# Taking the last 32 of 256 tokens out of the dense expert products of a PEER layer, and turning the output product

## The chip, the cores and the metric

The kernel runs on one core of one Trainium2 chip. The metric is the device time of one launch in microseconds (us), the median of several runs. The engines are TensorE (PE; PEld is its weight load), VectorE (DVE), ScalarE (ACT), GpSimd (POOL), and SyncE (SP), whose queue issues most DMAs.

## The reference

Two layers, each a trunk (attention, convolution and recurrence heads over 256 tokens of 1024 columns) and then a PEER mixer over 16384 experts of one neuron each. Only the mixer is touched by the change:

```python
def peer(xn, wq, k1, k2, u_tab, v_tab):
    q = (xt @ wq).reshape(t, PEER_HEADS, D_KEY)          # 8 heads
    ...
    v1, i1 = lax.top_k(s1, TOPK)                         # 16 of 128 keys, twice
    v2, i2 = lax.top_k(s2, TOPK)
    ...
    sv, ci = lax.top_k(cand, TOPK)                       # 16 of the 256 pairs
    experts = (e1 * N_KEYS + e2)                         # 128 experts a token
    gates = jax.nn.softmax(sv, axis=-1)
    ...
    hid = jax.nn.gelu(jnp.einsum("td,tkd->tk", xi, u_tab[ei]))
    return jnp.einsum("tk,tkd->td", gi * hid, v_tab[ei])
```

So each token needs the rows of 128 experts out of `u_tab` and out of `v_tab`. All is float32.

## The kernel before

**Dense instead of gathered.** The kernel multiplies all 256 tokens with all 16384 rows of `u` and of `v`, and a matrix of gates, zero where an expert was not chosen, stands between the two. A weight block is 128x1024 float32 (512 KB). `load` (L151, on SP's queue) brings it into one of three `raw` buffers; `split` makes of it two parts that TensorE takes at full rate, `hi` on ScalarE (L163) and `lo` on VectorE (L164), in three buffers each. `fixed_weight` (L168 to L174) multiplies the block with the 256 tokens: for each of eight 128x128 pieces hi by XH, hi by XL, and lo by XH, 24 matmuls of 256 columns.

**Stages of one layer's mixer.** Sixteen such blocks make the queries (`wq`), and scores with the keys come out of them. A list of tasks then finds the experts: `first_level` (L629, top 16 of 128, with `top16` L623 to L627), `second_prep` (L670), `second_level`, `decode_ranks` (L686 to L702), `decode_index`, `decode_sum` (L710, L717 to L721), `gates` and `turn` (L740 to L752, the transposed expert numbers `eH`, `eT` and gates `gT`), each for two halves `tt` of 128 tokens. Nearly all of it is VectorE's. The tasks are dealt out over the first J1 = 36 blocks of `u` (`hpair`, two blocks each). The other 92 blocks run beside 64 `quad`s: one quad builds, by comparisons on VectorE (L776, L782) and scaled copies on ScalarE and VectorE (L789, L792), one-hot matrices for four tokens and multiplies them in eight float16 matmuls (L798) into these tokens' columns of the gate matrix in `ab`. `hpair` also takes the gelu and the product with the gates.

Then comes the V stage: 128 `out_step`s, one for each block of `v`. ScalarE (L846) and VectorE (L847) split the coefficients of the block into two parts `chl`, which are the stationary operand here; `accumulate` (L250 to L252) runs 12 matmuls of 512 columns of `v` with them into four PSUM banks, which hold the output with tokens on partitions. `add_rows` adds the residual and takes the norm's sums.

**What sets the order.** The source is written in the order of these loops, but the instructions of each engine are ordered when the kernel is built, by a scheduler that may take an instruction earlier than it stands in the source when its inputs are there; `split` has a raised priority. Each engine then runs its own list in that order.

In the names below, `lo`, `hi`, `raw` are the block's parts, `ab` is the large buffer with the gates, the coefficients and the tasks' scratch, `cst` are constants.

Of the kernel before, what the change touches and what calls it, by code (L numbers as in the profile page):

```python
# [7 lines left out]
F32 = mybir.dt.float32  # L8
# [9 lines left out]
P = 128  # L18
# [17 lines left out]
CW = 661  # L36
# [9 lines left out]
def hymba_peer_kernel(  # L46
# [11 lines left out]
    v_in: bass.AP,  # L58
    g1_in: bass.AP,
# [15 lines left out]
    WARM=12,  # L75
):
# [25 lines left out]
    ab = one.tile([P, P * T], F32, name="ab")  # L102
    ab3 = ab.rearrange("p (n t) -> p n t", t=T)
# [37 lines left out]
    # products of zeros: the tensor engine's clock is up when the first rows arrive  # L141
# [44 lines left out]
    def add_rows(tt, ps, gb):  # L186
        # the residual, its rows' scales, and its product with the gains
# [76 lines left out]

    def log1p_exp_neg_abs(dst, z, n, tag):
# [3 lines left out]
        # exp(-|z|) = ((1 - t) / (1 + t)) ** 4 with t = tanh(|z| / 8)  # L269
# [8 lines left out]
        # log1p(e) = 2 atanh(e / (2 + e))  # L278
# [10 lines left out]
    def trunk(l, mx_p, prev, gb):  # L289
# [44 lines left out]
        # values and forget gates, in the layout [token, column]  # L334
# [41 lines left out]
        # log(1 + exp(-|z|)) of the forget gates and of the recurrence's lambda  # L376
# [9 lines left out]
        # cumulative log forget gates as rank-two terms of the logits  # L386
# [29 lines left out]
        # conformer convolution  # L416
# [19 lines left out]
        def layer_norm():  # L436
# [16 lines left out]
            # a Newton step: y (1.5 - 0.5 v y^2)  # L453
# [10 lines left out]
        # gated linear recurrence  # L464
# [30 lines left out]
        def rnn_scan():  # L495
            # -expm1(2 log_a) = tanh(-log_a) (1 + a^2)
# [10 lines left out]
            # sqrt(v) = v y (1.5 - 0.5 v y^2)  # L507
# [11 lines left out]
        # attention  # L519
# [61 lines left out]
        # output projection and residual  # L581
# [11 lines left out]
        return wq  # L593

    def peer(l, oh_p, wq, next_gain):
        o = 16384
# [22 lines left out]
        gT = oh_p.tile([P, 2, T], F32, name="gT", bufs=1)  # L619

# [83 lines left out]
        def decode_index(tt, s):  # L704
            # sum over ranks a of (a == chosen rank) * index[a]
# [31 lines left out]
        def turn(tt):  # L737
# [7 lines left out]
            # the scaled gate as two float16 parts, each kept as float32  # L745
# [8 lines left out]
        for tt in range(2):  # L754
# [11 lines left out]
            tasks.append((1.0, lambda tt=tt: turn(tt)))  # L766

# [41 lines left out]
        def hpair():  # L809
            j = jc[0]  # L810
            b = bank()
            fixed_weight(u_in[l, j], b[:, 0:T])
            fixed_weight(u_in[l, j + 1], b[:, T:2 * T])
            bv = b.rearrange("p (n t) -> p n t", t=T)
# [3 lines left out]
            else:  # L818
                hg = oh_p.tile([P, 2, T], F32, tag="hg", name="hg")
# [21 lines left out]
        def out_step(j):  # L841
            def f():
                chl = oh_p.tile([P, 2, T], F32R, tag="hg", name="chl")
# [6 lines left out]
                return (chl[:, 0, :], chl[:, 1, :]), w  # L850
# [11 lines left out]
        pr = [bankb() for _ in range(4)]  # L862
# [128 lines left out]
```

## Time and profile before

| | us |
|---|---|
| median of 3 runs | 1882.45 (1881.66 to 1882.49) |
| span of the profiled execution | 1879.8 |
| TensorE busy | 1850.7 (98%) |
| VectorE busy | 1358.5 (72%) |
| ScalarE busy | 1196.0 (64%) |
| POOL busy | 28.1 (1%) |
| mean DMA rate | 175 GB/s |

The profile comes from one execution. Its page gives busy time by engine, the chain of work that ended last, groups of instructions by line, and the DMA issues; the trace behind it can be asked for windows, single instructions and the chain in a stretch. A matmul's shown duration contains its way through the array, so the time from one start to the next, not the duration, tells how fast matmuls follow each other.

### The profile page before, as it was taken

The page shows a single profiled execution, that of the slowest core. Times are in us where ns is not written, and L with a number is a line of the kernel's source. Part 1 is how long each engine was busy: PE and PEld are TensorE (multiplying, and loading weights), DVE is VectorE, ACT ScalarE, POOL GpSimd, SP SyncE. Part 2 cuts the span into 40 slices and gives each one's busy share as a digit, 9 for nine tenths or more (in the row PEclk, how much of TensorE's full clock was granted, in tenths as well). Part 3 has the DMA queues.
Part 4 walks back from the last instruction along what each step waited for, and adds up shares of the span by engine and source line. Part 5 has one row for each costly group of instructions (what it writes and reads, how often), then busy time and mean ns, then how long its engine had stood idle before and what let it go on. Part 6 is the DMA issues. An engine that isn't in the chain of part 4 may idle for free.

```text
span 1879.8 us, 33413 instructions
## 1 busy us (share of the span) xinstructions
PE 1850.7 (98%) x12688; PEld 1672.3 (89%) x12688; DVE 1358.5 (72%) x2902; ACT 1196.0 (64%) x2345; POOL 28.1 (1%) x34
## 2 busy tenths in 40 slices
PE   9999999999999999999999999999999999999998
PEld 8889999999998888888897899999999988888886
DVE  6969987778885555555688699777788755555555
ACT  5954668888874444444469455598888744444444
POOL 0100000000000000000010000000000000000000
PEclk9999999999999999999999999999999999999999
DMA  6264555555555655555543545655555565555554
GB/s 228 91 210 154 168 184 168 160 167 166 163 166 202 211 188 186 188 190 188 184 156 118 174 152 172 193 160 166 168 159 169 167 213 191 186 187 189 190 190 136
DMA packets 90016, 328.86 MB, mean 175 GB/s; under 512 B 9984, under 2 KB 9984, under 8 KB 89600
## 3 DMA queue, kind: packets, MB, share of 16 engines
q1 hardware_dynamic: 88704, 322.54, 52.8%
q10 hardware_dynamic: 1152, 4.19, 0.6%
q8 instruction: 99, 1.62, 0.3%
q14 instruction: 61, 0.50, 0.1%
HBM read 323.55 MB, written 3.15 MB: 174 GB/s over the span
## 4 chain that ended last, share of the span: by engine, by line
PE 89%; DVE 8%; ACT 2%; issue 1%; POOL 0%; DMA 0%; POOLq 0%; SPq 0%; ACTq 0%
PE bank L172 14%; PE bank L174 14%; PE bank L173 14%; PE bankb L251 13%; PE bankb L250 13%; PE bankb L252 13%; PE bankb L798 3%; DVE lo L164 3%; PE bank L651 1%; DVE ab L627 1%; DVE ab L625 1%; DVE ab L626 1%; DVE ab L624 1%; PE bank L231 0%; DVE ab L623 0%
## 5 line engine op out<-in xcount | busy, mean ns | idle before, releaser
L164 DVE TENSOR_TENSOR lo<-raw,hi 128x1024 fp32r<-128x1024 f32 (+1 forms) x600 | 734.1, 1225 | 255.6 <-ACT hi L163 252.1
L163 ACT ACTIVATE hi<-raw 128x1024 fp32r<-128x1024 f32 (+1 forms) x600 | 630.5, 1053 | 262.8 <-PE bank L173 126.3
L172 PE MATMUL bank<-XH,hi 128*128 128x256 f32 x2560 | 732.0, 286 | 0.0
L174 PE MATMUL bank<-XH,lo 128*128 128x256 f32 x2560 | 723.0, 282 | 6.2 <-DVE lo L164 6.2
L173 PE MATMUL bank<-XL,hi 128*128 128x256 f32 x2560 | 719.5, 281 | 0.7 <-DVE XL L236 0.7
L174 PEld LDWEIGHTS bank<-XH,lo 128*128 128x128 f32 x2560 | 483.0, 189 | 8.4 <-DVE lo L164 8.2
L172 PEld LDWEIGHTS bank<-XH,hi 128*128 128x128 f32 x2560 | 484.4, 189 | 1.4 <-issue 0.4
L173 PEld LDWEIGHTS bank<-XL,hi 128*128 128x128 f32 x2560 | 483.5, 189 | 1.1 <-DVE XL L236 1.1
L250 PE MATMUL bankb<-hi,chl 128*128 128x512 f32 x1024 | 406.1, 397 | 1.0 <-ACT chl L846 1.0
L251 PE MATMUL bankb<-lo,chl 128*128 128x512 f32 x1024 | 405.5, 396 | 0.0
L252 PE MATMUL bankb<-hi,chl 128*128 128x512 f32 x1024 | 405.3, 396 | 0.0
L846 ACT ACTIVATE chl<-ab 128x256 fp32r<-128x256 f32 x256 | 106.7, 418 | 361.7 <-PE bankb L252 361.7
L789 ACT ACTIVATE ob<-oe,gT 128x128 f16<-128x128 f16 x768 | 251.9, 407 | 0.9 <-DVE oe L782 0.9
L250 PEld LDWEIGHTS bankb<-hi,chl 128*128 128x128 f32 x1024 | 192.7, 188 | 48.7 <-ACT chl L846 2.4
L252 PEld LDWEIGHTS bankb<-hi,chl 128*128 128x128 f32 x1024 | 192.1, 188 | 47.3 <-DVE chl L847 0.7
L251 PEld LDWEIGHTS bankb<-lo,chl 128*128 128x128 f32 x1024 | 192.6, 188 | 45.4
L847 DVE SCALAR_TENSOR_TENSOR chl<-ab,chl 128x256 fp32r<-128x256 f32 x256 | 108.9, 426 | 157.9 <-ACT chl L846 157.9
L776 DVE TENSOR_TENSOR oa<-iota,eH 128x512 f16<-128x512 f16 x128 | 54.2, 424 | 50.1 <-PE bankb L798 49.3
L798 PE MATMUL bankb<-ob,oa 128*128 128x128 f16 x1024 | 74.0, 222 | 0.0
L792 DVE TENSOR_SCALAR ob<-iota_h,eT,gT 128x128 f16<-128x128 f16 x256 | 70.6, 310 | 0.0
L782 DVE TENSOR_TENSOR oe<-iota,eH 128x512 f16<-128x512 f16 x128 | 53.9, 424 | 20.6 <-ACT ob L789 19.7
L798 PEld LDWEIGHTS <-oa 128*128 128x128 f16 x1024 | 60.2, 115 | 4.0
(198 smaller groups left out, 1171.4 us busy)
## 6 DMA issues: line engine op xcount, KB each, us to landing
raw<-in_u_dram SPq DMA_DIRECT2D x256, 512.0 KB, 3.5
raw<-in_v_dram SPq DMA_DIRECT2D x256, 512.0 KB, 4.2
raw<-in_ws_dram SPq DMA_DIRECT2D x32, 512.0 KB, 3.6
raw<-in_wq_dram SPq DMA_DIRECT2D x32, 512.0 KB, 4.0
raw<-in_wo_dram SPq DMA_DIRECT2D x16, 512.0 KB, 3.8
raw<-in_wv_dram SPq DMA_DIRECT2D x8, 528.0 KB, 3.7
ab<-in_g_dram SPq DMA_DIRECT2D x4, 512.0 KB, 5.8
ab<-in_kt_dram SPq DMA_DIRECT2D x2, 1024.0 KB, 6.7
```

The costliest lines, as they stand in the source:

```text
L163: S.activation(out=hi, in_=r, func=AF.Copy)
L164: V.tensor_tensor(out=lo, in0=r, in1=hi.bitcast(F32), op=ALU.subtract)
L172: TE.matmul(out=ps, lhsT=hi[:, k, :], rhs=XH[:, k, :], start=(k == 0), stop=False)
L173: TE.matmul(out=ps, lhsT=hi[:, k, :], rhs=XL[:, k, :], start=False, stop=False)
L174: TE.matmul(out=ps, lhsT=lo[:, k, :], rhs=XH[:, k, :], start=False, stop=(k == KT - 1))
L250: TE.matmul(out=po, lhsT=mh, rhs=hi[:, d0:d0 + 512], start=(m == 0), stop=False)
L251: TE.matmul(out=po, lhsT=mh, rhs=lo[:, d0:d0 + 512], start=False, stop=False)
L252: TE.matmul(out=po, lhsT=ml, rhs=hi[:, d0:d0 + 512], start=False, stop=(m == n - 1))
L789: S.activation(out=ob[:, s, i, :], in_=oe[:, :, i], func=AF.Copy, scale=gT[:, s, t:t + 1])
L798: TE.matmul(out=b[:, i * P:(i + 1) * P], lhsT=oa[:, :, i], rhs=ob[:, s, i, :], start=(s == 0), stop=(s == 1))
L846: S.activation(out=chl[:, 0, :], in_=c, func=AF.Copy, scale=1.0 / GS)
L847: V.scalar_tensor_tensor(out=chl[:, 1, :], in0=c, scalar=1.0 / GS, in1=chl[:, 0, :].bitcast(F32), op0=ALU.mult, op1=ALU.subtract)
```

## The change

For the last TG = 32 tokens the dense products are left out; TD = 224 tokens stay dense.

- `fixed_weight` on `u` blocks takes 224 columns of XH and XL; there are 56 quads instead of 64; `ab` holds 128 x 224 columns.
- `gathered_rows` lays the 32 tokens' normed rows out so that partition 32 g + t holds token t (`hG`, four copies). `gathered_index` makes expert numbers `idx` and gates `gG` in the same layout: on partition 32 g + t, column i, is expert 32 g + i of token t.
- `gathered_dot(i)`: an indirect DMA on POOL (L689) fetches, for each of the 128 partitions, the row of `u` of its expert in column i (4 KB a row, 512 KB in all) into one of NROW = 3 buffers; VectorE multiplies with `hG` and sums along the row into `cG` (L695). `gathered_gelu` applies gelu and gates. `gathered_sum(i)` fetches rows of `v` in the same way and adds them, scaled by `cG`, to `aG` (L707, L709). There are 32 dots and 32 sums a layer; the source places the dots among the 92 blocks of `u` and the sums among the steps of V.
- V is transposed: `accumulate_turned` has the pieces of `v` as the stationary operand, and for each of eight of them one matmul of 448 columns (hi with both parts of the coefficients) and one of 224 (lo). They fill all eight PSUM banks. At the end `finish` adds the two parts, transposes back, and adds `aG` by a matmul that sums the four groups.
- The tasks run for `tt` = 1 first, since the 32 tokens are in that half.

```diff
+    def accumulate_turned(ot, steps, tail, finish):
...
+            TE.matmul(out=ot[d][:, 0:2 * TD], lhsT=hi[:, w],
+                      rhs=chl.rearrange("p s t -> p (s t)"), start=(m == 0), stop=False)
+            TE.matmul(out=ot[d][:, 0:TD], lhsT=lo[:, w], rhs=chl[:, 0, :], start=False,
+                      stop=(m == n - 1))
...
+        def gathered_rows():
...
+            for dh in range(2):
+                b = bank()
+                TE.matmul(out=b, lhsT=dr, rhs=xg[:, dh * 512:(dh + 1) * 512],
+                          start=True, stop=True)
+                S.activation(out=hG[:, dh * 512:(dh + 1) * 512], in_=b, func=AF.Copy)
...
+        def fetch(src, i):
+            r = oh_p.tile([P, D], F32, tag="row", name="row", bufs=NROW)
+            G.indirect_dma_start(out=r, out_offset=None, in_=src,
+                                 in_offset=bass.IndirectOffsetOnAxis(ap=idx[:, i:i + 1], axis=0))
+            return r
+
+        def gathered_dot(i):
+            r = fetch(ur_in, i)
+            V.scalar_tensor_tensor(out=r, in0=r, scalar=1.0, in1=hG, op0=ALU.mult, op1=ALU.mult,
+                                   accum_out=cG[:, i:i + 1])
...
+        def gathered_sum(i):
+            r = fetch(vr_in, i)
+            c = cG[:, i:i + 1]
+            if i == 0:
+                aG.append(oh_p.tile([P, D], F32, tag="hG", name="aG", bufs=1))
+                V.tensor_scalar(out=aG[0], in0=r, scalar1=c, scalar2=None, op0=ALU.mult)
+            else:
+                V.scalar_tensor_tensor(out=aG[0], in0=r, scalar=c, in1=aG[0],
+                                       op0=ALU.mult, op1=ALU.add)
...
-        for tt in range(2):
+        for tt in (1, 0):
...
-            fixed_weight(u_in[l, j], b[:, 0:T])
-            fixed_weight(u_in[l, j + 1], b[:, T:2 * T])
+            fixed_weight(u_in[l, j], b[:, 0:TD], n=TD)
+            fixed_weight(u_in[l, j + 1], b[:, TD:2 * TD], n=TD)
...
+            while dots < TG and dots < (jp + 1) * TG / (rest - GLEAD):
+                gathered_dot(dots)
+                dots += 1
...
+        for i in range(TG):
+            j = 4 + i * (P - GTAIL) // TG
+            steps[j] = with_sum(i, steps[j])
...
+        def finish(d):
+            tb = carve(9 * D + (d % 2) * TD, TD)
+            S.activation(out=tb, in_=ot[d][:, TD:2 * TD], func=AF.Copy)
+            V.tensor_tensor(out=oT[:, d, :], in0=ot[d][:, 0:TD], in1=tb, op=ALU.add)
...
+            TE.transpose(y[dh][0][:, q * P:(q + 1) * P], oT[:, d, 0:P], ident)
+            TE.transpose(y[dh][1][0:P - TG, q * P:(q + 1) * P], oT[:, d, P:TD], ident)
```

The order in which the built program runs it differs from the order of the source. VectorE of before, in J1, in the middle of the tasks, where one `lo` (L164) stands after every nine or ten small instructions:

```order
L164 TENSOR_TENSOR lo<-raw,hi 128x1024
L627 MAX_INDEX ab<-ab 128x8
L624 MAX_INDEX ab<-ab 128x8
L625 MATCH_REPLACE ab<-ab 128x128
L670 TENSOR_TENSOR ab<-ab 128x8x8
L626 MAX ab<-ab 128x8
L670 TENSOR_TENSOR ab<-ab 128x8x5
L627 MAX_INDEX ab<-ab 128x8
L670 TENSOR_TENSOR ab<-ab 128x8x16
L661 CAST ab<-ab 128x256
L670 TENSOR_TENSOR ab<-ab 128x8x4
L164 TENSOR_TENSOR lo<-raw,hi 128x1024
```

VectorE of after, in J1, at the end of the tasks and then at the first dots (`lo` is L175 here; L803 to L814 are the last decoding instructions, L675 and L683 make `idx`, L841 to L845 are `turn`):

```order
L803 TENSOR_TENSOR ab<-iota_r,ab 128x2048 x2
L810 TENSOR_TENSOR ab<-ab 128x2048 x2
L175 TENSOR_TENSOR lo<-raw,hi 128x1024
L812 TENSOR_TENSOR ab<-ab 128x8x128 x2
L812 TENSOR_TENSOR ab<-ab 128x8x64 x2
L812 TENSOR_TENSOR ab<-ab 128x8x32 x2
L814 TENSOR_TENSOR ab<-ab 128x128 x2
L175 TENSOR_TENSOR lo<-raw,hi 128x1024 x10
L675 SCALAR_TENSOR_TENSOR ab<-ab 128x128
```

```order
L683 TENSOR_SCALAR idx<-bankb 128x32
L685 COPY gG<-bankb 128x32
L175 TENSOR_TENSOR lo<-raw,hi 128x1024
L695 SCALAR_TENSOR_TENSOR row,cG<-row,hG 128x1024 x4
L175 TENSOR_TENSOR lo<-raw,hi 128x1024
L695 SCALAR_TENSOR_TENSOR row,cG<-row,hG 128x1024 x6
L175 TENSOR_TENSOR lo<-raw,hi 128x1024
L695 SCALAR_TENSOR_TENSOR row,cG<-row,hG 128x1024 x5
L175 TENSOR_TENSOR lo<-raw,hi 128x1024
L695 SCALAR_TENSOR_TENSOR row,cG<-row,hG 128x1024 x6
```

The small work that stood between the `lo` of some thirty blocks is in front of ten `lo` in a row now: ahead of the first of these rows the `lo` of six neighbouring blocks have 65, 36, 27, 57, 26 and 8 instructions between them. The dots and, with the same spacing, the sums behind them all stand before the first quad; there are 13 `lo` among the 64.

POOL of before, and then of after, in the first layer, from the norm ahead of the mixer on (L183 and L195 are the norm's `ss`, L411 and L445 are the trunk's):

```order
L411 TENSOR_SCALAR ab<-ab,cst 16x256 x8
L183 TENSOR_TENSOR ss<-ss,cst 128x1 x2
L665 MEMSET ab 128x512 x2
L183 TENSOR_TENSOR ss<-ss,cst 128x1 x2
L411 TENSOR_SCALAR ab<-ab,cst 16x256 x8
```

```order
L195 TENSOR_TENSOR ss<-ss,cst 128x1 x2
L758 MEMSET ab 128x512 x2
L689 DMA row<-in_ur_dram,idx 128x1024 x32
L689 DMA row<-in_v_dram,idx 128x1024 x32
L195 TENSOR_TENSOR ss<-ss,cst 128x1 x2
L445 TENSOR_SCALAR ab<-ab,cst 16x256 x8
```

POOL's list gains the 64 gathers of a layer, one after the other, behind the memsets of the tasks and ahead of the next norm; a gather waits there until the dot or sum three places ahead has left its buffer.

## Rows read from the trace of the kernel before

**Rows 1.** Page: busy time by engine, then the chain that ended last.
```profile
PE 1850.7 (98%) x12688; PEld 1672.3 (89%) x12688; DVE 1358.5 (72%) x2902; ACT 1196.0 (64%) x2345; POOL 28.1 (1%) x34
...
PE 89%; DVE 8%; ACT 2%; issue 1%; POOL 0%; DMA 0%; POOLq 0%; SPq 0%; ACTq 0%
```

**Rows 2.** Busy time by stage: J1, U rest, V; second J1.
```profile
core 0: us, PE busy (x) PEld busy (x) DVE busy (x) ACT busy (x) POOL busy (x), PEclk, DMA share, GB/s
179.60:288.00 108.40, 105.24 (x882) 104.11 (x882) 97.15 (x364) 65.01 (x82) 0.00 (x0) 1.00 0.54 174
288.00:583.70 295.70, 295.70 (x2723) 293.34 (x2721) 228.05 (x449) 244.37 (x620) 0.00 (x0) 1.00 0.52 166
583.70:939.30 355.60, 355.10 (x1522) 285.44 (x1521) 210.94 (x261) 173.44 (x255) 0.00 (x0) 1.00 0.58 193
...
1111.00:1219.00 108.00, 104.97 (x874) 103.75 (x874) 97.10 (x364) 64.67 (x82) 0.00 (x0) 1.00 0.55 175
```

**Rows 3.** Timeline of TensorE in three places: start, duration, matmul.
```profile
20.32 0.28 PE L348 MATMUL bankb<-hi,XH 128*128 128x264 f32 x1
...
21.41 0.29 PE L348 MATMUL bankb<-hi,XH 128*128 128x264 f32 x1
...
310.03 0.28 PE L172 MATMUL bank<-XH,hi 128*128 128x256 f32 x1
...
310.62 0.28 PE L174 MATMUL bank<-XH,lo 128*128 128x256 f32 x1
...
699.73 0.40 PE L252 MATMUL bankb<-hi,chl 128*128 128x512 f32 x1
...
701.13 0.40 PE L252 MATMUL bankb<-hi,chl 128*128 128x512 f32 x1
```

**Rows 4.** Weight loads by shape, whole span: busy us, mean ns.
```profile
L172 PEld LDWEIGHTS bank<-XH,hi 128*128 128x128 f32 x2560 | 484.4, 189 | 1.4 <-issue 0.4
...
L569 PEld LDWEIGHTS bankb<-ab 128*64 128x64 f32 x32 | 3.7, 137 | 2.1
```

**Rows 5.** VectorE: `lo` in J1, its timeline there; one shape of L432.
```profile
L164 DVE TENSOR_TENSOR lo<-raw,hi 128x1024 fp32r<-128x1024 f32 x36 | 43.8, 1221 | 11.5 <-ACT hi L163 11.3 <-issue 0.2
...
184.47 1.21 DVE L164 TENSOR_TENSOR lo<-raw,hi 128x1024 fp32r<-128x1024 f32 x1
185.61 0.28 DVE L626 MAX8 ab<-ab 128x8 f32<-128x128 f32 x1
...
L432 DVE SCALAR_TENSOR_TENSOR ab<-ab,par 128x256 f32<-128x256 f32 x120 | 52.1, 485 | 0.3
```

**Rows 6.** DMA issues by tile (median us to landing); POOL by line.
```profile
raw<-in_u_dram SPq DMA_DIRECT2D x256, 512.0 KB, 3.5
...
ab<-in_kt_dram SPq DMA_DIRECT2D x2, 1024.0 KB, 6.7
...
L411 POOL TENSOR_SCALAR ab<-ab,cst 16x256 f32<-16x256 f32 x16 | 17.1, 1082 | 75.8 <-ACT ab L409 75.8
L183 POOL TENSOR_TENSOR ss<-ss,cst 128x1 f32<-128x1 f32 x10 | 8.7, 870 | 1739.1 <-DVE ss L181 1732.1 <-DMA cst<-in_cst_dram 7.0
```

**Rows 7.** The chain of waits in the U rest: start, duration.
```profile
300.50 0.93 PE bankb L798 x16
```

**Rows 8.** Windows at the start and the end: columns as in Rows 2.
```profile
10.00:15.00 5.00, 4.68 (x31) 4.40 (x30) 3.50 (x6) 2.78 (x6) 0.93 (x1) 0.79 0.78 306
15.00:20.00 5.00, 4.78 (x37) 4.45 (x37) 4.74 (x11) 3.55 (x4) 0.00 (x0) 1.00 0.40 138
1870.00:1880.00 10.00, 2.45 (x11) 1.66 (x9) 4.75 (x10) 3.50 (x8) 1.72 (x2) 0.79 0.28 105
```

More of the change, by code (lines that the diff above doesn't have):

```diff
@@ L35 @@
     0, 128, 256, 512, 640, 648, 656, 657, 658, 659, 660)
-CW = 661
+CSEL = 661
+TG = 32
+TD = T - TG
+NG = P // TG
+CW = CSEL + TG
+NX = P * P
 TRUNK = ("R Q0 C1 C0 t7 t4 t8 c K0 t1 g L0 Q1 L1 K1 P0 Q2 L2 L3 t1 G t10 P1 t2 t6 W0 P2 K2 S P3 L4 L5 W1 Q3 "
@@ L58, in hymba_peer_kernel @@
     v_in: bass.AP,
+    ur_in: bass.AP,
     g1_in: bass.AP,
@@ L75, in hymba_peer_kernel @@
     WARM=12,
+    NROW=3,
+    GLEAD=4,
+    GTAIL=12,
 ):
@@ L171, in fixed_weight @@
         for k in range(KT):
-            TE.matmul(out=ps, lhsT=hi[:, k, :], rhs=XH[:, k, :], start=(k == 0), stop=False)
-            TE.matmul(out=ps, lhsT=hi[:, k, :], rhs=XL[:, k, :], start=False, stop=False)
-            TE.matmul(out=ps, lhsT=lo[:, k, :], rhs=XH[:, k, :], start=False, stop=(k == KT - 1))
+            xh, xl = XH[:, k, 0:n], XL[:, k, 0:n]
+            TE.matmul(out=ps, lhsT=hi[:, k, :], rhs=xh, start=(k == 0), stop=False)
+            TE.matmul(out=ps, lhsT=hi[:, k, :], rhs=xl, start=False, stop=False)
+            TE.matmul(out=ps, lhsT=lo[:, k, :], rhs=xh, start=False, stop=(k == KT - 1))
     def small(shape, tag, dt=F32):
@@ L263, in accumulate, with block @@
                     one_half(n - tail + i, st, tt, (dh,))
+    def accumulate_turned(ot, steps, tail, finish):
+        n = len(steps)
+        def block(m, st, d):
+            chl, (hi, lo) = st
+            w = slice(d * P, (d + 1) * P)
+            TE.matmul(out=ot[d][:, 0:2 * TD], lhsT=hi[:, w],
+                      rhs=chl.rearrange("p s t -> p (s t)"), start=(m == 0), stop=False)
+            TE.matmul(out=ot[d][:, 0:TD], lhsT=lo[:, w], rhs=chl[:, 0, :], start=False,
+                      stop=(m == n - 1))
+        for m in range(n - tail):
+            st = steps[m]()
+            for d in range(KT):
+                block(m, st, d)
+        last = [steps[m]() for m in range(n - tail, n)]
+        for d in range(KT):
+            for i, st in enumerate(last):
+                block(n - tail + i, st, d)
+            finish(d)
     def log1p_exp_neg_abs(dst, z, n, tag):
@@ new lines, in gathered_index @@
+        def gathered_index():
+            e = ea[:, 1, 0, :]
+            V.scalar_tensor_tensor(out=e, in0=e, scalar=float(P), in1=ea[:, 1, 1, :],
+                                   op0=ALU.mult, op1=ALU.add)
+            b = bankb()
+            for g in range(NG):
+                for s in range(2):
+                    TE.matmul(out=b[g * TG:(g + 1) * TG, s * TG:(s + 1) * TG],
+                              lhsT=ident[:, P - TG:P],
+                              rhs=ea[:, 1, 2 * s, g * TG:(g + 1) * TG], start=True, stop=True)
+            V.tensor_scalar(out=idx, in0=b[:, 0:TG], scalar1=float(l * NX), scalar2=None,
+                            op0=ALU.add)
+            V.tensor_copy(out=gG, in_=b[:, TG:2 * TG])
@@ new lines, in gathered_gelu @@
+        def gathered_gelu():
+            S.activation(out=cG, in_=cG, func=AF.Gelu_apprx_tanh)
+            V.tensor_tensor(out=cG, in0=cG, in1=gG, op=ALU.mult)
+        def gathered_sum(i):
[6 more added lines that the diff above has]
+                V.scalar_tensor_tensor(out=aG[0], in0=r, scalar=c, in1=aG[0],
+                                       op0=ALU.mult, op1=ALU.add)
@@ L766, in peer @@
             tasks.append((1.0, lambda tt=tt: turn(tt)))
+            if tt == 1:
+                tasks.append((0.8, gathered_index))
         jc = [0]
@@ L854, in peer @@
         begun = []
+        dots = 0
         for jp in range(rest):
-            while tq[0] < T // 4 and tq[0] < (jp + 1) * (T // 4) / (rest - QLEAD):
+            while tq[0] < TD // 4 and tq[0] < (jp + 1) * (TD // 4) / (rest - QLEAD):
                 quad()
+            while dots < TG and dots < (jp + 1) * TG / (rest - GLEAD):
+                gathered_dot(dots)
+                dots += 1
             if jp >= rest - EARLY:
```

89 lines of the change are left out of this document (60 added, 29 removed).

## The prediction

> **What bounds the kernel now.** I read the page's busy shares first, then its chain, then the stage windows. TensorE is busy 1850.7 of 1879.8 us and holds 89% of the chain that ended last; the rest of the chain is VectorE with 8% and ScalarE with 2% [rows 1]. The windows cut each layer into three stages that the change touches: the 36 U blocks that run beside the top-16 tasks (I call it J1, 108.40 us), the other 92 U blocks with the 64 quads (295.70 us) and the V stage (355.60 us); the second layer repeats the first (J1 108.00 us) [rows 2]. TensorE is busy throughout the last two. In J1 the picture is tighter than the busy share of the whole kernel suggests: VectorE works 97.15 of the 108.40 us beside TensorE's 105.24. So TensorE sets the end of the U rest and of V, and J1 is a stage in which VectorE has only 11 us to spare. The profiled span is 1879.8 us, the median of the runs 1882.45 us; 2.65 us lie around the span and I keep them.
>
> **What the change takes from TensorE.** Successive 256-column matmuls start 0.118 us apart (five steps from 310.03 to 310.62), 264-column ones 0.121 us (nine steps from 20.32 to 21.41), 512-column ones 0.233 us (six steps from 699.73 to 701.13) [rows 3]. The line through 256 and 512 gives 0.45 ns a column, so 224 columns would take 0.1036 us and 448 columns 0.2045 us. A 128-column weight load takes 189 ns and a 64-column one 137 ns [rows 4]; 0.81 ns a column means that successive loads can hardly follow each other faster than some 104 ns, so the narrower matmul may be held by its load. Bounds for 224 columns: 0.1036 (the line goes on) and 0.118 (no gain at all); I take 0.106, nearest to both the line and the load. U rest: 92 blocks x 24 matmuls x 0.012 us = -26.5 us (between -31 and 0). Eight quads fewer: two quads' 16 matmuls stand in the chain with 0.93 us [rows 7], so 8 x 0.465 = -3.7 us. The quads' VectorE and ScalarE work that goes too was hidden beside TensorE and gives nothing. V: a step was 12 matmuls of 512 columns, 2.778 us of window; transposed it is eight pairs of 448 and 224 columns, 8 x (0.2045 + 0.106) = 2.484 us, for 128 steps 318.0 us, so -37.5 us (between -40 and -25). Together -67.7 us a layer: this is what the dots have to cost less than.
>
> **Where the dots go.** The source spreads 32 dots over the U rest and 32 sums over V, where VectorE has 68 and 145 us free in the windows of rows 2. The program that is built doesn't: the order of after has all 64 on VectorE in J1, right behind the gathered indices, in runs of four to six between two `lo`. A U block needs one `lo`, and the next `lo` stands behind five or six instructions that each wait for a gather. hi and lo have three buffers, so TensorE gets at most three blocks ahead and then waits for VectorE. The dots are on the path, not beside it.
>
> **J1 after, step by step.** It has three parts in the order.
> - The small top-16 and decode work, which in before stands a few instructions at a time between the `lo`, is now in front: between the `lo` of six neighbouring U blocks stand some 220 instructions, and behind them come about twelve `lo` with almost nothing between. VectorE's 97.15 us in J1 hold 43.8 us of `lo`, so the rest is 53 us [rows 2, 5]. With nine blocks' `lo` at the back-to-back pitch of 1.14 us (184.47 to 185.61) it takes 53 + 9 x 1.14 = 63, I take 64 us, set by VectorE.
> - Twelve blocks at TensorE's pace: 12 x 24 x 0.106 = 30.5 us.
> - 64 dots and sums with 13 `lo` in their gaps. A row buffer is free when the dot on it ends; then POOL issues the gather for the dot three places on. With three buffers one round is gather plus dot, and brings three rows. The trace has no gather. A 512 KB load, the same bytes in the same 4 KB pieces, lands 3.5 us after SP issues it; the slowest load of the rows, 1024 KB of keys, takes 6.7 us [rows 6]. POOL's own small instructions take 0.87 to 1.08 us [rows 6], and it has to do one for each gather. I take 3.5 + 1.0 = 4.5 us for the gather, with bounds 3.5 and 6.7, because its size is that of the first row and POOL's part comes on top. A dot has the size of `lo`, 1.22 us [rows 5]. Period (4.5 + 1.2)/3 = 1.9 us, 64 x 1.9 = 121.6 us; the `lo` fit into the waiting.
> - Two blocks behind them: some 4 us.
>
> Sum 64 + 30.5 + 121.6 + 4 = 220 us against 108.4, so +111.7 us. A rule of the Trainium skill would make it less: its page "DMA: Bandwidth & Descriptors", section "Anatomy of one DMA — SWDGE (gpsimd) path", fits 2.0 us plus bytes over 436 GB/s for a DMA that POOL issues, 3.2 us here; by that estimate the total would be near 1935 us. The trace has no such DMA to set beside it.
>
> **The small terms.** The gathered rows' two matmuls and copies behind wq block 4: +1 us. TensorE waits for most of J1 after; the rows show a granted clock of 0.79 behind slow starts, and 1.00 five us later [rows 8]. While VectorE sets the pace a lower clock costs nothing; when TensorE sets it again, some 10 us at 0.79, at the end of the first part and of the third, cost 2 us each: +4 us (0 to 8). The tail of V: 16 transposes, two small matmuls and, for the last of the eight blocks, a ScalarE copy, a VectorE add and two transposes in a chain; by the 0.12 us of a 256-column matmul and the 0.485 us of a 256-column VectorE instruction [rows 3, 5] +5 us (2 to 8). The 64 gathers are 32 MB a layer at a DMA share of 0.54 [rows 2], spread over 120 us: hidden, except that raw loads share the same engines.
>
> Per layer: +111.7 - 26.5 - 3.7 - 37.5 + 1 + 4 + 5 = +54.0 us; two layers +108 us. Profiled span 1988, median about **1990 us**.
>
> **Rivals.**
> *The gathers keep up.* If the gather of a row lands before VectorE comes to it (about 2.2 us a gather or less, or a landing that doesn't stretch with the load), the dots run at `lo`'s pitch: 64 x 1.14 + 13 x 1.14 = 88 us instead of 121.6. J1 is 186 us, a layer +20 us, the total 1923 us, and with the better ends of all the other terms 1889 us. For it: DMA has half its time free in J1. Against it: no load of that size in the trace lands in under 3.5 us, and POOL is slow. 15%.
>
> *The gathers are slower still.* At 6.7 us a row costs 2.6 us, J1 is 267 us and the total about 2085 us; at 8 us 2140. For it: POOL issues all 64 in one queue, each for 128 separate rows, beside raw loads, and VectorE is never long idle there. The Trainium skill speaks for it, "SBUF — State Buffer", section "SBUF: two separate sides": POOL's descriptors wait while VectorE holds the shared port. No run here shows it yet, and POOL has 34 instructions in the whole trace. 15%.
>
> *The other side: faster.* One mechanism: VectorE passes the 64 rows so quickly that J1 grows by less than the 67.7 us which the narrower products give. With wq, clock and tail as above J1 may grow 58 us, which leaves 0.82 us a row; with the best ends (-74.8 us and nothing for the small terms) 1.09 us. At 1.0 us a row and those ends, J1 is 177 us, a layer -6 us and the total 1871 us. Against it: the pitch of `lo` is 1.14 us without any wait, and chained VectorE instructions of a quarter of the size already take 0.485 us [rows 5]. 4%.
>
> *The change doesn't do what its diff says*, that is the dots do run beside TensorE's work. This would give 2 x (-67.7 + 10), 1767 us. The order speaks plainly against it: 2%.
>
> **How the numbers follow.** Forecast (a row in 1.6 to 2.2 us, total 1950 to 2060): 64%. The range takes in most of the fast-gather case (from 1915) and of the slow one up to 6.7 us a gather: 1915 to 2080. What is left out is fast gathers with good TensorE ends and the other side below, gathers of over 6.7 us or no gain in U above, together 2 in 10. About 0.2% (4 us) is what a measurement of this kernel can tell from no change. Faster: 4%, from the two last rivals, less what the first of them leaves within that bound; same 3%; slower 93%.
>
> **What would show it.** In the windows of after: J1 near 220 us with TensorE under half busy, U rest near 265, V near 318. On VectorE the 64 dots at 1.9 us each, ended by a wait for the gather, not back to back; TensorE idle before `lo`. Matmuls of 224 columns 0.106 us apart, of 448 columns 0.2045. In the chain VectorE and the gathers take the place of TensorE for some 110 us a layer. I am wrong if the dots run back to back (first rival), if a gather takes over 6.7 us (second), if 224 columns start 0.118 apart, or if J1's first part is not the 64 us of small work.

## The result, and the profile after

The changed kernel takes **2161.81 us** (2158.64 to 2162.64, four runs), before 1882.47 us: a ratio of 1.148, interval 1.1466 to 1.1498. The direction was right, the size was not: +279 us instead of +108, above the range's end of 2080.

The page of after, its busy shares and its chain, to be laid beside [rows 1]:

```profile
span 2156.8 us, 35955 instructions
...
PE 1868.3 (87%) x13664; PEld 1746.2 (81%) x13664; DVE 1467.4 (68%) x3040; ACT 1157.2 (54%) x2253; POOL 187.5 (9%) x162
...
PE 75%; DMA 7%; DVE 7%; issue 6%; POOL 3%; ACT 2%; POOLq 0%; DVEq 0%; SPq 0%; ACTq 0%
```

TensorE is busy 87% of the time, not 98%, and it isn't even busy for less time: 1868 us against 1851, although 32 of 256 columns are gone: V has more matmuls (x2070 in its window, x1522 in before), and those of J1 run partly at a lower clock. The chain now holds gathers, POOL and "issue" with 16% together. The windows of the first layer, cut at the same places as [rows 2] (J1 in four parts: tasks, blocks at TensorE's pace, dots, rest; then U rest, then V to the next norm), say where:

```profile
core 0: us, PE busy (x) PEld busy (x) DVE busy (x) ACT busy (x) POOL busy (x), PEclk, DMA share, GB/s
181.80:239.70 57.90, 31.36 (x181) 29.99 (x180) 57.40 (x312) 22.00 (x22) 0.00 (x0) 0.72 0.17 56
239.70:269.90 30.20, 30.20 (x278) 30.05 (x278) 16.14 (x20) 14.26 (x19) 0.12 (x1) 0.98 0.65 197
269.90:434.00 164.10, 65.17 (x338) 62.58 (x337) 94.20 (x110) 18.27 (x23) 79.28 (x64) 0.64 0.74 246
434.00:446.90 12.90, 12.90 (x95) 12.90 (x94) 8.17 (x18) 5.20 (x13) 0.00 (x0) 0.80 0.64 203
446.90:723.00 276.10, 275.85 (x2659) 274.45 (x2659) 213.93 (x411) 228.12 (x569) 0.00 (x0) 1.00 0.56 176
723.00:1080.70 357.70, 347.17 (x2070) 307.69 (x2069) 202.89 (x277) 176.13 (x271) 0.87 (x1) 1.00 0.61 195
```

In the first row VectorE is busy 57.4 of 57.9 us and TensorE half of it: the tasks stand in front. In the second the picture turns over. In the third nobody is busy: TensorE 65 of 164 us, VectorE 94, POOL 79, DMA 0.74; everyone waits for someone. The fourth is TensorE at a granted clock of 0.80, behind a stretch with 0.64.

The three stages by kernel, in us. They are cut at the first matmul of 224 columns (of before and of u256, below: the first block of `u`), the first quad, the first matmul of V and the norm behind it:

| first layer | J1 | U rest | V to norm | median of the runs |
|---|---|---|---|---|
| before | 107.8 | 294.2 | 360.4 | 1882 |
| after | 265.6 | 276.1 | 357.7 | 2161.8 |
| nodots: no gathers, dots, sums (the 32 tokens' part is left out) | 136.2 | 276.0 | 358.0 | 1901.4 |
| nodots_tasks: also tasks behind each latest `lo` | 119.0 | 276.9 | 357.7 | 1867.0 |
| nodots_hg3: nodots with three `chl` buffers | 137.5 | 275.9 | 333.0 | 1851.2 |
| pin: dots and sums where the source has them | 136.7 | 284.9 | 360.5 | 1929.9 |
| u256: after, U blocks with 256 columns | 116.0 | 299.4 | 357.9 | 1908.6 |
| best1: pin, tasks spread, three `chl`, two row buffers | 118.2 | 287.5 | 338.4 | 1847.5 |

### The profile page after: what moved, and what is told of

Same layout as the page of the kernel before. It is cut to its first block, busy times and chain, and to the rows that moved or that the text cites. A ratio compares the mean times of both kernels' runs of the same rounds, so it can differ in the third digit from the quotient of the medians.

```text
span 2156.8 us, 35955 instructions
## 1 busy us (share of the span) xinstructions
PE 1868.3 (87%) x13664; PEld 1746.2 (81%) x13664; DVE 1467.4 (68%) x3040; ACT 1157.2 (54%) x2253; POOL 187.5 (9%) x162
## 4 chain that ended last, share of the span: by engine, by line
PE 75%; DMA 7%; DVE 7%; issue 6%; POOL 3%; ACT 2%; POOLq 0%; DVEq 0%; SPq 0%; ACTq 0%
PE bank L184 12%; PE bank L186 12%; PE bank L185 12%; PE bankb L284 11%; PE bank L284 10%; DMA row<-in_v_dram,idx 5%; PE bank L286 5%; PE bankb L286 5%; POOL row L689 3%; PE bankb L893 2%; DVE lo L175 1%; DMA row<-in_ur_dram,idx 1%; PE bank L744 1%; DVE ab L718 1%; PE bankb L264 1%
## 5 line engine op out<-in xcount | busy, mean ns | idle before, releaser
L175 DVE TENSOR_TENSOR lo<-raw,hi 128x1024 fp32r<-128x1024 f32 (+1 forms) x600 | 734.3, 1225 | 439.1 <-ACT hi L174 431.0
L186 PE MATMUL bank<-XH,lo 128*128 128x224 f32 (+1 forms) x2560 | 746.7, 292 | 236.2 <-DVE lo L175 236.2
L184 PE MATMUL bank<-XH,hi 128*128 128x224 f32 (+1 forms) x2560 | 750.6, 293 | 12.7 <-ACT hi L174 12.7
L185 PE MATMUL bank<-XL,hi 128*128 128x224 f32 (+1 forms) x2560 | 739.8, 289 | 0.7 <-DVE XL L248 0.7
L284 PE MATMUL bankb<-chl,hi 128*128 128x448 f32 x1024 | 354.6, 390 | 12.4 <-DVE chl L942 5.0
L284 PE MATMUL bank<-chl,hi 128*128 128x448 f32 x1024 | 339.5, 376 | 0.0
L286 PE MATMUL bank<-chl,lo 128*128 128x224 f32 x1024 | 272.3, 266 | 0.0
L286 PE MATMUL bankb<-chl,lo 128*128 128x224 f32 x1024 | 272.2, 266 | 0.0
L284 PEld LDWEIGHTS bankb<-chl,hi 128*128 128x128 f32 x1024 | 191.9, 187 | 66.4 <-DVE chl L942 48.3
L286 PEld LDWEIGHTS bank<-chl,lo 128*128 128x128 f32 x1024 | 195.1, 191 | 0.0
L286 PEld LDWEIGHTS bankb<-chl,lo 128*128 128x128 f32 x1024 | 195.1, 190 | 0.0
L195 POOL TENSOR_TENSOR ss<-ss,cst 128x1 f32<-128x1 f32 x10 | 8.6, 861 | 1434.2 <-DVE ss L193 1427.0
L695 DVE SCALAR_TENSOR_TENSOR row<-row,hG 128x1024 f32<-128x1024 f32 x64 | 77.9, 1226 | 72.7 <-DMA row<-in_ur_dram,idx 72.3
L709 DVE SCALAR_TENSOR_TENSOR aG<-row,cG,aG 128x1024 f32<-128x1024 f32 x62 | 79.7, 1285 | 62.7 <-DMA row<-in_v_dram,idx 61.8
L689 POOL DMA_INDIRECT row<-in_ur_dram,idx x64 | 79.9, 1249 | 337.3 <-DVE gG L685 259.3
```

The costliest lines, as they stand in the source:

```text
L175: V.tensor_tensor(out=lo, in0=r, in1=hi.bitcast(F32), op=ALU.subtract)
L184: TE.matmul(out=ps, lhsT=hi[:, k, :], rhs=xh, start=(k == 0), stop=False)
L185: TE.matmul(out=ps, lhsT=hi[:, k, :], rhs=xl, start=False, stop=False)
L186: TE.matmul(out=ps, lhsT=lo[:, k, :], rhs=xh, start=False, stop=(k == KT - 1))
L284: TE.matmul(out=ot[d][:, 0:2 * TD], lhsT=hi[:, w], rhs=chl.rearrange("p s t -> p (s t)"), start=(m == 0), stop=False)
L286: TE.matmul(out=ot[d][:, 0:TD], lhsT=lo[:, w], rhs=chl[:, 0, :], start=False, stop=(m == n - 1))
```

## The experiments

The stages differ by layer in a few us at most, so two layers make the totals. Every kernel builds on the changed one.

### Are the dots dear, or their place?

```diff
+            last_lo[0] = V.tensor_tensor(out=lo, in0=r, in1=hi.bitcast(F32), op=ALU.subtract)
...
+            with tc.issue_after(last_lo[0].ins):
+                V.scalar_tensor_tensor(out=r, in0=r, scalar=1.0, in1=hG, ...)
```

> The changed kernel, with each dot and sum of VectorE put where the source has it: behind the latest lo, so the dots lie among the last 92 U blocks and the sums among the steps of V. Theory PLACE (the loss is that lo stands behind waits for gathers in the J1 stage): the 164 us which 64 rows and 13 lo took fall to 15 blocks of 2.67 us, 40 us; about -137 us a layer, total 1890 us, up to 1970 us if the sums lengthen V by up to 1.28 us each. Rival GATHER (a gather costs VectorE time wherever it runs, since POOL's issue and VectorE exclude each other): some 0.94 us for each of 64 rows stays, +60 us a layer on that: 1950 to 2030 us.

**Measured** 1929.9 us, ratio to before 1.0254 (1.0229 to 1.0279): 232 us less than after, by order alone; the same gathers and the same arithmetic run. The windows (J1, U rest, V):

```profile
181.00:317.70 136.70, 111.28 (x890) 109.61 (x889) 99.15 (x362) 60.17 (x75) 3.99 (x4) 0.86 0.47 151
317.70:602.60 284.90, 281.25 (x2658) 276.62 (x2657) 245.49 (x474) 229.07 (x569) 29.03 (x31) 1.00 0.72 229
602.60:963.10 360.50, 350.13 (x2070) 307.76 (x2069) 239.40 (x309) 176.09 (x271) 49.40 (x30) 1.00 0.71 235
```

Beside TensorE's work 32 dots cost 8.9 us (284.9 against 276.0 without them, nodots below) and 32 sums 2.5 us; in the second layer 9.5 and 9 us, in all 28 us of the total. So PLACE, and the gathers as such are cheap: POOL's busy time here is what it was (82 us a layer, 80 in after).

The other way to the same question, to leave the gathers, dots and sums out:

```diff
-            r = fetch(ur_in, i)
-            V.scalar_tensor_tensor(out=r, in0=r, scalar=1.0, in1=hG, ...)
...
-            r = fetch(vr_in, i)
...
-                V.scalar_tensor_tensor(out=aG[0], in0=r, scalar=c, in1=aG[0],
-                                       op0=ALU.mult, op1=ALU.add)
```

> The changed kernel without the gathers, the 64 dots and sums of a layer: the contribution of the 32 gathered tokens is left out, all else stays. What the rest of the change is worth: by the trace of after J1 would be 58 us for its first nine blocks, 30 us for twelve and 40 us for fifteen, 128 us (before 108), U rest 276 (before 296), V and tail 358 (before 358): the total is about that of before, 1885 us. If the narrower products did gain what was forecast, 1800 us.

**Measured** 1901.4 us, ratio 1.0101 (1.0084 to 1.0118), 16 us above what was expected, since J1 takes 136 us and not 128. That is the finding of the study: even with nothing gathered, the kernel is slower than before. U rest gains 18 us, V 2.4 us, and J1 loses 28 us. The 260 us from here to after are the bunched dots and sums; the other 19 us are lost without any dot.

### Why did tasks and dots move?

In after and nodots, whose U blocks have 224 columns, the tasks lie in front of a row of `lo`, and in after the dots behind them; in before, with 256 columns, the tasks lie spread. So the columns alone were changed:

```diff
-            fixed_weight(u_in[l, j], b[:, 0:TD], n=TD)
-            fixed_weight(u_in[l, j + 1], b[:, TD:2 * TD], n=TD)
-            bv = b[:, 0:2 * TD].rearrange("p (n t) -> p n t", t=TD)
+            fixed_weight(u_in[l, j], b[:, 0:T])
+            fixed_weight(u_in[l, j + 1], b[:, T:2 * T])
+            bv = b.rearrange("p (n t) -> p n t", t=T)[:, :, 0:TD]
```

> The changed kernel, but U blocks are multiplied with all 256 columns (the 32 further columns of each result are not read); nothing else is edited, and nothing is pinned. In the order of the built program the tasks are then spread over J1 again and the dots and sums stand among the U rest's quads. Theory SHAPE: it is the 224-column shape that made the builder's scheduler put tasks and dots in front of lo; J1 108 to 115 us, U rest 295 to 305, V and tail 358: total 1885 to 1910 us, 250 us below the changed kernel although TensorE has more to do. Rival GATHER: the gathers cost wherever they are, 1950 us or more.

**Measured** 1908.6 us, ratio 1.0139 (1.0122 to 1.0156). SHAPE: TensorE gets 14% more columns in U and the kernel is 253 us faster than after. J1 takes 116 us (115 at most was expected), and it holds 17 gathers already; the dots and sums run spread from 244.8 to 491.5 us:

```profile
180.00:296.00 116.00, 107.78 (x898) 105.41 (x898) 110.03 (x383) 61.07 (x72) 25.21 (x17) 1.00 0.66 230
296.00:595.40 299.40, 297.78 (x2656) 292.43 (x2656) 267.66 (x486) 231.52 (x574) 65.40 (x47) 0.99 0.73 249
```

The move of the instructions hangs on the matmul's shape in U. Which price of the scheduler turns there was not looked at: open.

The tasks alone, without dots, by the same edit as pin on the tasks:

```diff
-                tasks[ti_][1]()
+                with tc.issue_after(last_lo[0].ins):
+                    tasks[ti_][1]()
```

> The run without gathers, dots and sums, with the tasks' VectorE work put behind the latest lo, so that it spreads over the J1 blocks. Theory BUNCH: the tasks in front of the lo cost TensorE 28 us a layer in J1 (136 us against 108 of before); spread, J1 falls to 105 to 118 us, total 1840 to 1865 us. Rival: J1 is long for another reason (quads or the turn wait): 1900 us.

**Measured** 1867.0 us, ratio 0.9923 (0.9906 to 0.9939): 34 us less than nodots, all in J1 (136 to 119). BUNCH holds, just short of its range (1865, and 118 in J1). It gives back 17 of the 28 us that J1 had lost. In what is left TensorE waits 12 us for `lo` and `hi` (3 in before), and its granted clock is 0.94; what sets those waits is open.

### What sets the pace of the bunched dots?

One round of after, from the first dot on: dot (L695), POOL's gather (L689), `lo`; start and duration, and in brackets how long the engine was idle ahead of it and for whom. The last line is the last sum (L709):

```profile
275.21 1.23 DVE L695 SCALAR_TENSOR_TENSOR row<-row,hG 128x1024 f32<-128x1024 f32 x1 [4.06 <-DMA row<-in_ur_dram,idx]
...
276.72 0.94 POOL L689 DMA_INDIRECT row<-in_ur_dram,idx  x1 [3.27 <-DVE row L695]
277.77 1.23 DVE L695 SCALAR_TENSOR_TENSOR row<-row,hG 128x1024 f32<-128x1024 f32 x1 [1.32 <-DMA row<-in_ur_dram,idx]
...
279.04 1.23 DVE L695 SCALAR_TENSOR_TENSOR row<-row,hG 128x1024 f32<-128x1024 f32 x1
279.27 1.80 POOL L689 DMA_INDIRECT row<-in_ur_dram,idx  x1 [1.62 <-DVE row L695]
...
281.38 1.72 POOL L689 DMA_INDIRECT row<-in_ur_dram,idx  x1 [0.30 <-issue]
...
282.21 1.22 DVE L175 TENSOR_TENSOR lo<-raw,hi 128x1024 fp32r<-128x1024 f32 x1
...
283.49 0.55 PE L186 MATMUL bank<-XH,lo 128*128 128x224 f32 x1 [5.84 <-DVE lo L175]
...
284.42 1.23 DVE L695 SCALAR_TENSOR_TENSOR row<-row,hG 128x1024 f32<-128x1024 f32 x1 [0.98 <-DMA row<-in_ur_dram,idx]
...
433.02 1.28 DVE L709 SCALAR_TENSOR_TENSOR aG<-row,cG,aG 128x1024 f32<-128x1024 f32 x1
```

A dot waits for its row, POOL for the dot that frees a buffer, TensorE for the `lo` behind the dots. From the first dot (275.2) to the end of the last sum (434.3) are 159.1 us, 2.49 us a row, and three rows make a round of 7.46 us. (The expectation for two buffers, below, counts to 431.9, where the last sum but one ends: 157 us, 2.45 and 7.35 us.) The gather itself lands 5.3 us (median) after its issue begins:

```profile
row<-in_ur_dram,idx POOLq DMA_INDIRECT x64, 5.3
row<-in_v_dram,idx POOLq DMA_INDIRECT x64, 5.2
```

Two theories of the rest: buffers only divide a fixed latency, or POOL's issue and VectorE's instruction keep each other out. The row at 279.27 speaks for the second: POOL's issue takes 0.94 us when VectorE is idle and ends 0.8 us after the dot when it begins inside one. Of the 64 issues of this stretch 23 took 1.3 us or more (all but one 1.66 to 1.93) and all of them began inside a VectorE instruction of 1.2 us; of the 41 shorter ones 32 did not, six began in the last 0.03 us of one and three (1.01 to 1.20 us) in its last 0.4 us. The Trainium skill, "SBUF — State Buffer", section "SBUF: two separate sides", names such a lock between the two engines, held by whichever starts first. The rows agree with it on one side only: POOL waits, while a dot that starts inside an issue (at 305.87, in the issue of 305.68) keeps its 1.23 us, as all dots here (1.22 to 1.23). The lock costs 23 times 0.8 us, 19 of the 159 us, so it isn't the whole.

A first try with six buffers, three of them in an unused part of the large buffer, told nothing: later blocks write that part, so half of the gathers of `u` waited for quads, and as the part holds coefficients too, a part of the computation is changed.

```diff
+            if count[0] % 6 < 3:
...
+                r = carve((6 + count[0] % 6) * D, D)
```

> The changed kernel with six row buffers instead of three (three of them in a part of the large buffer that is unused then), order of the dots unchanged. Theory LATENCY (a row costs gather plus dot, divided by the buffers): VectorE becomes the limit, 1.15 us a row and 0.25 us for its share of lo, 64 rows in 90 us instead of 164, total about 2014 us. Rival EXCLUSION (POOL's 0.94 us of issue and VectorE's 1.15 us can't overlap): 2.3 us a row as before, some 150 us, total 2130 us or more.

**Measured** 2202.7 us; with this edit no verdict. Five real buffers, and then two:

```diff
-    NROW=3,
-    NSPL=3,
+    NROW=5,
+    NSPL=2,
```

> The changed kernel with five row buffers instead of three; to make room, hi and lo have two buffers instead of three, which slows the U rest and V, so only the stretch with the dots is read. LATENCY: a round of 7.5 us now brings five rows, 1.5 us a row, the 64 rows and their lo take 96 to 110 us instead of 164. EXCLUSION (POOL's issue of 0.94 us and VectorE's instructions can't overlap): 2.1 to 2.4 us a row, 135 to 155 us.

**Measured** between the two: from the first dot to the end of the last sum 120.6 us (286.0 to 406.6), 1.88 us a row, a round of 9.4 us; the gathers now land 6.3 to 6.5 us after issue, at a DMA share of 0.89. (The total, 2158.8 us, is that of after: with two buffers each for `hi` and `lo` the U rest takes 293 us instead of 276, and the stages ahead of J1 are longer too.)

```profile
281.00:411.00 130.00, 61.82 (x314) 59.27 (x314) 93.54 (x110) 16.42 (x22) 87.88 (x64) 0.63 0.89 314
...
row<-in_ur_dram,idx POOLq DMA_INDIRECT x64, 6.5
...
286.04 1.22 DVE L695 SCALAR_TENSOR_TENSOR row<-row,hG 128x1024 f32<-128x1024 f32 x1 [3.72 <-DMA row<-in_ur_dram,idx]
...
405.35 1.28 DVE L709 SCALAR_TENSOR_TENSOR aG<-row,cG,aG 128x1024 f32<-128x1024 f32 x1
```

Both rivals fall in their pure form. From 7.46 us for three and 9.42 us for five rows a round would be 4.5 us and 0.98 us more for each row (4.3 and 1.03 in the expectation). That was then put to a test with two:

> The changed kernel with two row buffers instead of three. From three buffers (2.45 us a row, a round of 7.35 us) and five (1.88 us, 9.4 us) a round is 4.3 us plus 1.03 us for each row in it. ROUND: two buffers make a round of 6.35 us, 3.2 us a row, 64 rows in 204 us instead of 157, total about 2255 us. SLOT (a buffer's own cycle is 7.35 us whatever their number): 3.7 us a row, 236 us, total 2320 us.

**Measured** 2250.4 us, and from the first dot to the end of the last sum 217.0 us (276.7 to 493.8), 3.39 us a row, a round of 6.78 us:

```profile
276.74 1.23 DVE L695 SCALAR_TENSOR_TENSOR row<-row,hG 128x1024 f32<-128x1024 f32 x1 [5.01 <-DMA row<-in_ur_dram,idx]
...
492.47 1.28 DVE L709 SCALAR_TENSOR_TENSOR aG<-row,cG,aG 128x1024 f32<-128x1024 f32 x1 [0.45 <-DMA row<-in_v_dram,idx]
```

ROUND's total of 2255 us is met, but its stretch of 204 us is not: 13 us more. That the total came right is luck: the stretch grew by 58 us in the first layer, not by 47, but its last sums run beside the first quads (from 489.1 us on), so J1 and the U rest together grew by 46. SLOT, by which a round keeps its length whatever the number of buffers, falls too: a round takes 6.8, 7.5 and 9.4 us with two, three and five. So it has a large fixed part and grows with the rows in it, by 0.7 us for the third and 0.98 for each of the next two; the straight line is off by 0.3 us (5%) at two buffers. Whether the part that is served one after the other is POOL's issue (0.94 us) alone or also the DMA engines, which near their limit with five buffers, these runs don't separate; row5 also has fewer buffers for `hi` and `lo`.

### Why did V gain nothing?

The matmuls do go near the forecast pace: in after a pair of 448 and 224 columns takes 0.316 us (0.3105 forecast). But every second step has a hole, here ahead of 800.30. ScalarE's and VectorE's rows of the same stretch stand first, then TensorE's:

```profile
797.62 1.06 ACT L174 ACTIVATE hi<-raw 128x1024 fp32r<-128x1024 f32 x1 [1.50 <-PE bank L284]
...
798.71 1.23 DVE L175 TENSOR_TENSOR lo<-raw,hi 128x1024 fp32r<-128x1024 f32 x1 [1.31 <-ACT hi L174]
799.86 0.39 DVE L942 SCALAR_TENSOR_TENSOR chl<-ab,chl 128x224 fp32r<-128x224 f32 x1
...
799.75 0.37 PE L284 MATMUL bank<-chl,hi 128*128 128x448 f32 x1
799.96 0.27 PE L286 MATMUL bank<-chl,lo 128*128 128x224 f32 x1
800.30 0.47 PE L284 MATMUL bankb<-chl,hi 128*128 128x448 f32 x1
800.61 0.27 PE L286 MATMUL bankb<-chl,lo 128*128 128x224 f32 x1
```

`hi` waits for TensorE to end a step, `lo` for `hi`, and `chl` of the next step but one stands behind this `lo` on VectorE: 2.8 us from the end of one step, and only one step of 2.53 us lies in between. In before a step was 2.78 us and just covered it, if its chain was as long; that wasn't measured there.

```diff
-                chl = oh_p.tile([P, 2, TD], F32R, tag="hg", name="chl")
+                chl = oh_p.tile([P, 2, TD], F32R, tag="hg", name="chl", bufs=3)
```

> The run without gathers, dots and sums (their tokens' contribution is left out, as there), with three chl buffers instead of two. Theory CHAIN: V doesn't go at its matmuls' 2.53 us a step because chl of a step stands on ScalarE and VectorE behind hi and lo of a later block, which wait for a step of TensorE to end: 1.06 + 1.14 + 0.38 us and the handovers, 2.85 us, against one step of 2.53. With the third buffer V takes 128 x 2.53 = 324 us instead of 347, -22 us a layer, total 1857 us. Rival: V's pace is that of the matmul pairs themselves and the bubbles move elsewhere, total 1900 us.

**Measured** 1851.2 us, ratio 0.9836 (0.982 to 0.9853): CHAIN. V to norm takes 333 us instead of 358, 25 us a layer. In its rows the steps follow without a hole, eight pairs in 2.50 us:

```profile
799.59 0.37 PE L284 MATMUL bank<-chl,hi 128*128 128x448 f32 x1
...
802.09 0.37 PE L284 MATMUL bank<-chl,hi 128*128 128x448 f32 x1
```

### Why did U gain less?

```diff
-            TE.matmul(out=ps, lhsT=hi[:, k, :], rhs=xl, start=False, stop=False)
-            TE.matmul(out=ps, lhsT=lo[:, k, :], rhs=xh, start=False, stop=(k == KT - 1))
+            m = min(n, 192) if n < T else n
+            TE.matmul(out=ps[:, 0:m], lhsT=hi[:, k, :], rhs=xl[:, 0:m], ...)
+            TE.matmul(out=ps[:, 0:m], lhsT=lo[:, k, :], rhs=xh[:, 0:m], ...)
```

> The run without gathers, dots and sums, and two of three matmuls of a U block take 192 columns instead of 224 (the correction products of 32 more tokens are left out). LOAD: successive matmuls start 0.111 us apart because the weight load sets the pace, so nothing changes: U rest 276 us, spacing 0.111. COLUMNS: at 0.45 ns a column the two start 0.0144 us closer: U rest 276 - 92 x 16 x 0.0144 = 255 us.

**Measured** 1902.1 us beside nodots' 1901.4, U rest 275.4 us beside 276.0: LOAD. Two thirds of the matmuls lost 32 columns and nothing moved. In its rows three matmuls take 0.33 us, 0.111 each, as in after (0.111 from 600.01 to 601.46, thirteen steps):

```profile
499.86 0.29 PE L184 MATMUL bank<-XH,hi 128*128 128x224 f32 x1
499.99 0.26 PE L186 MATMUL bank<-XL,hi 128*128 128x192 f32 x1
500.08 0.27 PE L187 MATMUL bank<-XH,lo 128*128 128x192 f32 x1
500.19 0.29 PE L184 MATMUL bank<-XH,hi 128*128 128x224 f32 x1
```

What stays constant there is the 128-column load ahead of each. The Trainium skill, "TensorE: Matmul & The Clock Gate", section "LDWEIGHTS (loading the stationary operand)", gives such a load as its columns over 1.2 GHz, an estimate of 107 ns; the measured 0.111 us lies just above it, though the load's own shown duration is 189 ns [rows 4]. That it is the load, and not another fixed cost of an fp32 matmul, no run here separates. What is shown is that the columns don't count below 224, and the trace of before had it already. There, ahead of the mixer, 128 columns take no less: 13 steps in 1.45 us (1.73 less the last one's 0.28), 0.111 each:

```profile
123.70 1.73 PE L231 MATMUL bank<-dg,ab 128*128 128x128 f32 x14
```

### A version that beats both

Dots and sums pinned, tasks spread, `chl` with three buffers, rows with two to make room (dots are some 9 us apart there, so two suffice):

> As pin, and the tasks' VectorE work is put behind the latest lo too (so it spreads over J1 again), chl has three buffers instead of two, and the rows two instead of three to make room. PLACE: J1 as before, about 105 us; U rest 276; V at the pace of its matmuls, 128 x 2.53 = 324 us, tail +9; -45 us a layer, total about 1792 us. If the sums' 1.28 us still stand in V's way, up to 1870 us. GATHER: 1900 us.

**Measured** 1847.5 us, ratio to before 0.9815 (0.9797 to 0.9832): 314 us below the changed kernel and 34 below before. It misses the 1792 forecast, in J1 (118 us, not 105), in the U rest (287.5, not 276) and in V (338, not 333).

```profile
181.80:300.00 118.20, 106.85 (x889) 104.60 (x889) 106.63 (x404) 59.14 (x70) 4.59 (x3) 0.94 0.51 164
300.00:587.50 287.50, 282.20 (x2657) 276.91 (x2657) 247.16 (x480) 230.56 (x575) 29.03 (x31) 1.00 0.73 229
587.50:925.90 338.40, 328.44 (x2071) 307.96 (x2069) 237.54 (x309) 174.78 (x271) 50.03 (x31) 1.00 0.75 252
```

VectorE is busy 107 of 118 us in J1. Two tries at that; first the tasks behind every `lo` instead of every second:

```diff
-            hpair()
+            some_tasks(2 * jp + 1)
+            hpair(lambda: some_tasks(2 * jp + 2))
```

> As best1, with the tasks dealt out behind each lo instead of every second one. In best1 J1 took 118 us with 224 columns, while 36 blocks at TensorE's pace take 96. Theory BUNCH: pairs of lo with some 18 instructions ahead still make TensorE wait; J1 falls to 100 to 108 us, total 1820 to 1830 us. Rival: VectorE's 97 us of work in J1 and the waits at turn set J1, total 1845 us as best1.

**Measured** 1845.8 us, ratio 0.981 (0.9794 to 0.9826): the rival's total holds (J1 120 us, U rest 285), and the grain of the spreading isn't the point. What does set J1 there is not shown. Then more blocks:

```diff
-    J1=36,
+    J1=44,
```

> As best1, with J1 = 44 blocks instead of 36 for the tasks. In best1 J1 has VectorE busy 107 of 118 us while 36 blocks need TensorE for 96, so VectorE sets J1. BALANCE: over 44 blocks VectorE needs 53 + 44 x 1.22 = 107 us and TensorE 118, so J1 is about 122 to 128 us for eight blocks more, and the U rest is 84 blocks in about 268 us: J1 and U rest 390 to 396 us instead of 406, total 1825 to 1837 us. Rival: the U rest with its 32 dots and 56 quads is at VectorE's limit too (247 of 288 us busy), so what J1 gains is given back: 1845 us.

**Measured** 1856.6 us, ratio 0.9871 (0.9855 to 0.9888). J1 and U rest together are 408.7 us beside 405.7 of best1: J1 takes 137 us, not 122 to 128, and what the U rest gained was given back whole, and a little more. BALANCE falls; the rival comes nearer.

## Why the prediction was wrong, step by step

By layer, forecast and measured (from the windows; in J1 the gap makes 46 of the 85 us by which a layer was missed, or 42 if the forecast's clock term of 4 us is counted there):

| step | forecast | measured |
|---|---|---|
| tasks in front of `lo` | 64 | 57.9 |
| twelve blocks at TensorE's pace | 30.5 | 30.2 |
| 64 rows | 121.6 | 164.1 |
| blocks behind them | 4 | 12.9 |
| J1 against before | +111.7 | +157.8 |
| U rest against before | -30.2 | -18.1 |
| V with its tail against before | -32.5 | -2.7 |
| sum, with wq and clock | +54 | +139 |

- **What was right.** That the order of the program, not the source, decides; that tasks and dots stand in front of `lo` in J1; the first two rows of the sum to 6 us and 0.3 us; that TensorE then waits for VectorE and VectorE for gathers. u256, pin and nodots confirm it: 232 to 260 us hang on the place of the dots.
- **The 64 rows: mis-sized, the largest miss.** Two steps of the term failed. "3.5 + 1.0 = 4.5 us for the gather" took the landing of a plain load and added POOL's share; the gather lands in 5.3 us. (The 3.5 us is a median, not the least as the first rival has it: the quickest load of `u` landed in 3.2. The 3.2 us a gather named beside the sum falls shorter still.) And "one round is gather plus dot" gives 6.5 us even with that landing, 2.17 us a row; measured are 7.46 us, since issues and dots of the three rows queue behind each other and a third of the issues is lengthened beside VectorE. 1.9 us a row became 2.49, and the first landing, 5.4 us, came ahead of it. The upper bound of 6.7 us, 2.6 us a row, held it.
- **Blocks behind them.** Four blocks, not two, and at a granted clock of 0.80 as the clock term had it: 95 matmuls at 0.111 us are 10.5 us, they took 12.9, so 2.4 us of the clock term's 4.
- **U rest: the choice of 0.106.** The load was named as a possible limit and its time taken from a difference of two durations, 104 ns. It is 0.111 us: (0.111 - 0.106) x 92 x 24 = 11 us of the gap of 12. The row of 128-column matmuls shown above stood in the trace of before and would have said so.
- **V: the step whose mechanism failed.** "8 x (0.2045 + 0.106) = 2.484 us" was right to 2% as a sum of matmuls (2.53 measured) and wrong as a step, which took 2.70 on average. Nothing was said on what must be late next when a step gets shorter than the way of `hi`, `lo` and `chl`; nodots_hg3 shows that it was this way. -37.5 became about -12, and the tail added 9 us (1069.0 to 1080.7, in before 939.3 to 942.0) instead of 5. The -12 lies outside its own bound of -25.
- **The range.** Three terms erred to one side: with J1's upper bound (2.6 us a row) the forecast's own sum gives 2085, and the bounds of U and V, which were named, had not been added to it. The case "slower still" came true, though not by its condition of a gather of over 6.7 us.

## What to carry to other kernels

- Before a matmul is made narrower, look at what ends just behind it now: a stage that is bound by TensorE by a hair gains only until its next chain, here 2.8 us of `hi`, `lo`, `chl` where a step was 2.78 us, and one more buffer was worth 25 us a layer where V's narrowing and transposition without it had given 2.7.
- When a builder orders the instructions, read its order after every change of a shape, and pin what must lie beside other work to an instruction there: the same dots and sums cost 260 us in front of `lo` and 28 us beside the quads and the steps of V.
- Work that waits for DMA belongs on an engine's queue only where nothing that TensorE needs stands behind it.

## What the runs showed of the hardware

- In runs of equal fp32 matmuls, a 128-column load ahead of each, a matmul starts 0.111 us after the one before on average, whether 128, 192 (two of three) or 224 columns follow; 256 columns take 0.118 [rows 3]. An eighth fewer columns gave 6%. It is no floor of every 128-column load: the quads' float16 matmuls of 128 columns start 0.058 us apart (16 in 0.93 us [rows 7]).
- An indirect gather of 128 rows of 4 KB takes 0.94 us of POOL and lands 5.2 to 5.3 us after its issue begins (4.2 to 8.0), 6.3 to 6.5 us with five in flight. An issue that begins inside a 1.2 us VectorE instruction mostly takes 1.7 to 1.9 us and ends 0.8 us behind that instruction; VectorE's instruction isn't lengthened.
